# Hybrid decoder trunk: output-projection rows parked in DRAM through the expert stage, two more weight buffers, returned rows on SP's queue

## Chip, cores and metric

One core of one Trainium2 chip runs the whole kernel. The metric is the device time of one execution in microseconds; before the change it is 566.47 us (median of 3 runs, 566.22 to 566.54).

## What is computed

The reference, cut to what matters here (512 tokens, width 1024, 32 experts of which each token takes two):

```python
h = x + mix @ w_out                                   # output projection, mix from three mixers
h = h + hier_moe(rmsnorm(h, norm2_g), ...)            # 2 of 32 gated-MLP experts per token
gate = sigmoid(rmsnorm(h, ple_norm_g) @ ple_gate_w + ple_gate_b)
h = h + gate * (p @ ple_proj_w)
return rmsnorm(h, final_norm_g)
```

All is float32, and each expert's three matrices are 1024x256, 1024x256 and 256x1024: 3 MB an expert, 96 MB in all, read once.

## The kernel before

Tokens lie in four blocks `t` of 128 rows. `mixers` computes the mixers and adds the output projection to x; the sums stay in four SBUF tiles `h1[t]` of 128x1024 (4 KB a partition each). The rest is `ffn`, in these stages.

**Routing.** For each block, `route` (a generator, L782 on) normalizes h1[t], writes the normalized rows to DRAM tensor `tnd` by a DMA on the ACT queue (L790), and chooses experts. `spread` multiplies h1 by a selection to make the first expert pair's input; it is the last reader of h1 before the tail.

**Expert stage.** A loop over 16 pairs of experts, `i` = 0 to 15. `gate_up(i)` (line L997) multiplies by the two gate/up matrices, `down(i)` (L1029) by the two down matrices. A pair's output rows are scattered by token into DRAM tensor `yd` with an indirect DMA on POOL (L1043), for all pairs but the last; the next pair's input rows are gathered from `tnd` (L943).

**The weight stream.** The 96 MB come in 96 units of 1 MB. `load_units` (L691) takes a free buffer (a "slot") from the list `ring`, first in, first out, and issues the unit's DMA on SP's queue. SP's instructions stand in program order, so an issue that waits for a slot holds back all behind it. A manual dependency makes each unit wait until the third unit before it has landed, so three are in flight at most (`AHEAD = 3`). `free` puts slots back after each half of a pair. A pair's six units come in the order gate/up first halves, gate/up second halves, down, down.

**The end of the expert stage.** After `down(14)`, SP issues four 1 MB loads of the gate weights (`gate_load`, L1060) and two broadcast rows (L1190, L1191). POOL issues the four `load_y(t)` (L1162), each 1 MB: the two rows per token that the experts returned, read back from `yd`. They wait for the last scatter to land. From pair 14 on, the order on ACT and DVE is the program's, written by hand.

**The hand-over.** After `down(15)`: `add_y(0)` adds y's two rows to h1[0] (L1158, DVE, two instructions); `scatter` adds the last pair's output through two matmuls (L1051) and two DVE adds (L1053); `turn(0, hf)` transposes h1[0] (L1213) and copies it out (ACT L1215, DVE L1216). Between them stand twelve leftover steps of the per-layer embedding, `ple(4)` three times (PE L724, ACT copy L735). `split_gate(k, hf)` splits a piece of the raw gate weights into a high part (ACT L1068) and a low part (DVE L1069): 16 pieces, k = 0 to 7 for each half of the columns. Four are done ahead of the last `ple(4)`, twelve behind it. Then come the sigmoid table's load (L1309), `rms(0)` (ACT L1221, DVE L1202) and the tail: four blocks of gate matmuls (L1234), `finish` and the output. Blocks 1 to 3 get their `add_y` and `scatter` inside the tail.

The splits are the piece of code that the order of the end hangs on:

```python
    down(15, behind_down)              # behind_down: split_gate(0..2, 0), add_y(0)
    ple(PLE_LAST[0])
    for hf in range(2):
        scatter(hf)
    split_gate(3, 0)
    ple(PLE_LAST[1])
    lo = [turn(0, hf) for hf in range(2)]
    ple(PLE_LAST[2])
```

Of the kernel before, what the change touches and what calls it, by code (L numbers as in the profile page):

```python
# [38 lines left out]
def bcast(ap, parts=P):  # L39

    return bass.AP(tensor=ap.tensor, offset=ap.offset, ap=[[0, parts]] + [list(a) for a in ap.ap])
# [47 lines left out]
def mixers(ctx, tc, A, K, dbg):  # L89
# [360 lines left out]
    sbctx.close()  # L450
    pctx.close()
    hp = ctx.enter_context(tc.tile_pool(name="hp", bufs=1, side="left"))
    h1 = K["h1"] = [hp.tile([P, D], F32, name=f"h1_{t}") for t in range(NT)]
    for t in range(NT):
        nc.sync.dma_start(h1[t], A["x"][t * P:(t + 1) * P, :])
    parts = (step for t in range(NT) for hf in range(2) for step in out_proj(nc, K, mixh, mixl, hf, t, WO_EARLY))
# [157 lines left out]
def ffn(ctx, tc, A, K, mixh, mixl, out, dbg, stage):  # L614
# [21 lines left out]
    def unit(dt, shape, slot=None):  # L636
        slot = slot or ring.pop(0)
        u = slot[0].tile(shape, dt, name="unit", tag=slot[1])
        slot_of[id(u)] = slot, u
        return u  # L640
# [41 lines left out]

    slab, loads = {}, []

    def load_units(m=96):

        while ring and m and len(slab) < 96:
            n, m = len(slab), m - 1
            n = n - n % 6 + (0, 3, 1, 4, 2, 5)[n % 6]
            slab[n] = unit(F32, [P, 2048])  # L690
            loads.append(nc.sync.dma_start(slab[n], A["w_exp"][n // 3, n % 3]).ins)  # L691
            if len(loads) > AHEAD:
                tc.add_manual_dep(loads[-1], loads[-1 - AHEAD].name,
                                  mybir.DependencyInfo(mybir.DependencyClass.Sync, mybir.DependencyReason.DATA))
# [15 lines left out]
    def ple_load():  # L710
        pl_in.extend((big(0), unit(F32, [P, 2, D])))
        nc.sync.dma_start(pl_in[0], A["pT"])
        nc.sync.dma_start(pl_in[1], A["ple_proj_w"])

    def ple_steps():

        pT, pW = pl_in
        for j in range(8):
            t, hf = j // 2, j % 2
            p = ps("pe", "sc")  # L720
            for c in range(2):
                for k in range(2):
                    n = hf * 512 + c * 256
                    PE.matmul(p[:, c * 256:c * 256 + 256], pT[:, k * S + t * P:k * S + (t + 1) * P], pW[:, k, n:n + 256],  # L724
                              start=(k == 0), stop=(k == 1))
                    if c == k == 1:
                        kept.append((t, hf, p))
                        ple_out()
                    yield
# [9 lines left out]
    def ple(n):  # L739
        for _ in range(n):  # L740
            next(ple_left, None)
# [2 lines left out]
    V.tensor_copy(cm.rearrange("p a b -> p (a b)"), cmf)  # L744
    V.tensor_tensor(rw, rw, g2c[:, :, None].to_broadcast([P, KC, 36]), ALU.mult)
    tnd = dram.tile([S, D], F32, name="tnd")
    Ab = mw.tile([P, NT, 32], BF, name="Ab")
    pr_ = cw.tile([P, 448], F32, name="pr", tag="cmf")
    posA = pr_[:, :128].rearrange("p (t e) -> p t e", t=NT)
# [32 lines left out]
    def route(t):  # L782

        (ms2, hT, pl), ms = rt_in[t], small("ms", 1)
        V.tensor_tensor(ms, ms2[:, 0:1], ms2[:, 1:2], ALU.add)
        V.tensor_scalar(ms, ms, 1.0 / D, EPS, ALU.mult, ALU.add)
        r = rt_r[t] = rsqrt_cols(nc, mw, ms, 1, f"rs2{t}", K)
        tn = big(t % 2)
        SC.activation(tn, h1[t], AF.Copy, scale=r)
        nc.scalar.dma_start(tnd[t * P:(t + 1) * P, :], tn)  # L790
        yield

        lg = small("lg", 32)
        V.scalar_tensor_tensor(gp[:, t, :4], pl[:, :4], r, rb[:, :4], ALU.mult, ALU.add)
        V.scalar_tensor_tensor(lg, pl[:, 4:36], r, rb[:, 4:], ALU.mult, ALU.add)
        yield
        g8, gi = small("g8", 8, bufs=3), small("gi", 8, U32)
        V.max(g8, gp[:, t])
        yield
        V.max_index(gi, g8, gp[:, t])  # L800
        yield
        gf, oh = small("gf", 1), small("oh4", 4)
        V.tensor_scalar(gf, gi[:, 0:1], 8.0, None, ALU.mult)
        yield
        V.tensor_scalar(oh, iota32[:, 0:32:8], gf, None, ALU.is_equal)
        yield

        pr, ein = small("pr", 32), small("ein", 8)
        V.tensor_tensor(pr.rearrange("p (g e) -> p g e", g=4), lg.rearrange("p (g e) -> p g e", g=4),
                        oh[:, :, None].to_broadcast([P, 4, 8]), ALU.mult)  # L810
        yield
        V.tensor_reduce(ein, pr.rearrange("p (g e) -> p e g", g=4), AX, ALU.add)
        yield
        e8, ei = small("e8", 8, bufs=3), small("ei", 8, U32)
        V.max(e8, ein)
        yield
        V.max_index(ei, e8, ein)
        yield
        id2 = small("id2", 2, bufs=3)
        V.tensor_scalar(id2, ei[:, 0:2], gf, None, ALU.add)  # L820
        yield

        c0 = small("c0", 32, bufs=3)
        V.tensor_scalar(c0, iota32, id2[:, 0:1], None, ALU.is_equal)
        yield
        V.scalar_tensor_tensor(Ab[:, t], iota32, id2[:, 1:2], c0, ALU.is_equal, ALU.add)
        chosen[t] = g8, e8, id2, c0
# [104 lines left out]
    def one_hot(i, t):  # L932

        if t == 0:
            Dm[i] = mw.tile([P, NT, 2, 64], BF, name="Dm", tag="Dm")
        V.tensor_tensor(Dm[i][:, t], iota64[:, None, :].to_broadcast([P, 2, 64]),
                        posA[:, t, 2 * i:2 * i + 2, None].to_broadcast([P, 2, 64]), ALU.is_equal)
# [120 lines left out]
    def gate_load(j):  # L1058
        gr.append(unit(F32, [P, 4, 512]))
        nc.sync.dma_start(gr[j], A["ple_gate_w"][j])  # L1060

    def split_gate(k, hf):

        if hf == 0:
            gw[k] = unit(F32R, [P, 2, D])
        hs = slice(hf * 512, hf * 512 + 512)
        raw, h, l = gr[2 * hf + k // 4][:, k % 4], gw[k][:, 0, hs], gw[k][:, 1, hs]
        SC.activation(h, raw, AF.Copy, scale=g3c[:, k:k + 1])  # L1068
        V.scalar_tensor_tensor(l, raw, g3c[:, k:k + 1], h.bitcast(F32), ALU.mult, ALU.subtract)  # L1069
        if k % 4 == 3:  # L1070
            free(gr[2 * hf + k // 4])
# [3 lines left out]
    with tc.manual_schedule(engines={mybir.EngineType.DVE}):  # L1075
        run(steps[0])
        for t in (0, 1):
            hot_rms(t)
        logits(NT - 1, 1)
        run(steps[1], 3)  # L1080
        position(NT - 2)
        spread(0)
        run(steps[1], 2)
        hot_rms(NT - 2)
        spread(1)
        run(steps[1])
        spread(2)
        position(NT - 1)
        hot_rms(NT - 1)
        for t in range(3):  # L1090
            one_hot(1, t)
        spread(NT - 1)
        for hf in range(2):
            gather_T(0, hf)
        one_hot(1, NT - 1)
    ple_load()
    load_units()

# [56 lines left out]
    def add_y(t, rs=(0, 1)):  # L1155

        for r in rs:
            V.tensor_tensor(h1[t], h1[t], ys[t][:, r], ALU.add)  # L1158

    def load_y(t):  # L1160
        ys.append(unit(F32, [P, 2, D]))
        nc.gpsimd.dma_start(ys[t], yd.rearrange("(r n) d -> n r d", r=2)[t * P:(t + 1) * P])  # L1162

    ends = ExitStack()
    for i in range(16):
        if i == 14:
            ends.enter_context(tc.manual_schedule(engines={mybir.EngineType.Activation, mybir.EngineType.DVE}))
        gate_up(i, between(i))
        free(slab[6 * i + 1], slab[6 * i + 4])
        if i == 15:  # L1170
            break
        if i in (3, 7):
            eo.append(unit(F32, [P, 2, D]))
            ple_out()
        load_units()
        if i == 0:
            ple(PLE[0])
        gather_T(i + 1, 1)
        if i > 0:
            ple(PLE[i])  # L1180
        down(i, lambda n: gather_T(i + 1, 0))
        free(slab[6 * i + 2], slab[6 * i + 5])
        load_units()
        if i == 14:
            for t in range(NT):
                load_y(t)
            for j in range(4):
                gate_load(j)
            rows = mix.tile([P, 2, D], F32, name="rows", tag="m0")
            nc.sync.dma_start(rows[:, 0], bcast(A["ple_gate_b"]))  # L1190
            nc.sync.dma_start(rows[:, 1], bcast(A["final_norm_g"]))  # L1191


    free(slab[92], slab[95])
# [85 lines left out]
        for hf in range(2):  # L1280
            scatter(2 * t + hf)

    def behind_down(n):
        if n == 0:
            for k in range(3):
                split_gate(k, 0)
            add_y(0, (0,))
        if n == 1:
            add_y(0, (1,))

    down(15, behind_down)
    ple(PLE_LAST[0])
    for hf in range(2):
        scatter(hf)
    split_gate(3, 0)
    ple(PLE_LAST[1])
    lo = [turn(0, hf) for hf in range(2)]
    ple(PLE_LAST[2])
    free(pl_in[1])
    for f in lo:  # L1300
        f()
    for k in range(4, KC):
        split_gate(k, 0)
    count_beyond()
    for k in range(KC):
        split_gate(k, 1)
    ov_slots = ring[:3]
    junk, h3s = (unit(F32, shape, slot) for shape, slot in zip(([P, 2, 512], [P, 4, 512]), ring[3:]))
    SC.preload_act_table_set("sigmoid_and_others")  # L1309
# [160 lines left out]
```

## Time and profile before

| | us |
|---|---|
| median of 3 runs | 566.47 |
| the profiled execution, its own time | 564.66 |
| its span, first to last instruction | 562.9 |
| PE busy in the span | 517.0 |
| DVE busy | 276.7 |
| ACT busy | 210.6 |

Times in the rows count from the start of the span, on the slowest (here the only) core. PE is TensorE's matmuls, PEld its weight loads; an engine's name with a q is its instruction queue. The profiled execution lies 1.81 us below the median of the runs, and its span 1.76 us below its own time. The granted TensorE clock is 0.983 of full speed over the span.

### The profile page before, as it was taken

The page shows a single profiled execution, that of the slowest core. Times are in us where ns is not written, and L with a number is a line of the kernel's source. Part 1 is how long each engine was busy: PE and PEld are TensorE (multiplying, and loading weights), DVE is VectorE, ACT ScalarE, POOL GpSimd, SP SyncE. Part 2 cuts the span into 40 slices and gives each one's busy share as a digit, 9 for nine tenths or more (in the row PEclk, how much of TensorE's full clock was granted, in tenths as well). Part 3 has the DMA queues.
Part 4 walks back from the last instruction along what each step waited for, and adds up shares of the span by engine and source line. Part 5 has one row for each costly group of instructions (what it writes and reads, how often), then busy time and mean ns, then how long its engine had stood idle before and what let it go on. Part 6 is the DMA issues. An engine that isn't in the chain of part 4 may idle for free. (4 is left out here: it accounts for less than half of the span.)

```text
span 562.9 us, 7588 instructions
## 1 busy us (share of the span) xinstructions
PE 517.0 (92%) x2713; PEld 325.5 (58%) x2713; DVE 276.7 (49%) x735; ACT 210.6 (37%) x443; POOL 90.3 (16%) x126
## 2 busy tenths in 40 slices
PE   8999999999999999999999999988798897659992
PEld 5797886877996888853333333332223332448872
DVE  6663966847745667673222232221211112487764
ACT  7466765555856444211121111111011113173352
POOL 3301121311009300011111121100111002011110
PEclk9999999999999999999999999999999999788998
DMA  9881222300549589989999999999999999900111
GB/s 312 272 315 55 75 80 75 86 1 2 146 164 421 198 322 421 334 343 397 411 414 418 392 381 376 374 399 381 391 392 419 419 412 418 401 6 0 39 47 69
DMA packets 35641, 148.82 MB, mean 264 GB/s; under 512 B 6557, under 2 KB 14109, under 8 KB 22160
## 3 DMA queue, kind: packets, MB, share of 16 engines
q1 hardware_dynamic: 28896, 133.26, 61.8%
q0 software_dynamic: 5408, 12.15, 5.5%
q10 hardware_dynamic: 1296, 2.89, 1.3%
q8 instruction: 23, 0.38, 0.3%
q14 instruction: 18, 0.15, 0.1%
HBM read 139.61 MB, written 16.25 MB: 277 GB/s over the span
## 5 line engine op out<-in xcount | busy, mean ns | idle before, releaser
L997 PE MATMUL gu<-unit,xT 128*64 128x512 f32 x512 | 127.6, 598 | 12.4 <-DMA unit<-in_w_exp_dram 12.2
L997 PEld LDWEIGHTS gu<-unit,xT 128*64 128x64 f32 x512 | 37.1, 136 | 84.0 <-issue 59.0
L1029 PE MATMUL dn<-unit,hidT 128*64 128x512 f32 x256 | 61.0, 599 | 1.7 <-ACT hidT L1020 0.8
L234 PE MATMUL pj<-xh,wp 128*128 128x512 f32 x176 | 51.2, 398 | 0.4 <-ACT wp L69 0.4
L1234 PE MATMUL pg<-unit 128*128 128x512 f32 (+1 forms) x216 | 47.4, 376 | 1.1 <-ACT unit L1215 1.1
L1002 ACT ACTIVATE sg<-gu 128x256 f32<-128x256 f32 x16 | 6.2, 385 | 110.6 <-PE gu L997 110.6
L1003 DVE SCALAR_TENSOR_TENSOR hid<-sg,wsl,gu 128x256 f32<-128x256 f32 x16 | 7.7, 479 | 79.7 <-ACT sg L1002 79.7
L1234 PEld LDWEIGHTS pg<-unit 128*128 128x128 f32 x216 | 37.7, 192 | 9.0 <-ACT unit L1215 1.6
L1043 POOL DMA_INDIRECT yd<-big,idy x15 | 15.2, 1013 | 164.4 <-ACT big L1033 164.4
L1029 PEld LDWEIGHTS dn<-unit,hidT 128*64 128x64 f32 x256 | 19.1, 136 | 33.1 <-issue 24.5
L234 PEld LDWEIGHTS pj<-xh,wp 128*128 128x128 f32 x176 | 32.5, 188 | 8.0 <-ACT wp L69 1.1
L1033 ACT ACTIVATE big<-dn 128x512 f32<-128x512 f32 x30 | 17.9, 597 | 50.5 <-PE dn L1029 50.5
L930 DVE COPY SL<-sl 128x10 f32<-128x10 f32 (+1 forms) x17 | 2.9, 168 | 66.4 <-PE sl L929 66.4
L70 DVE TENSOR_TENSOR wp<-wraw,wp 128x768 fp32r<-128x768 f32 (+2 forms) x28 | 25.8, 928 | 13.7 <-ACT wp L69 13.4
L69 ACT ACTIVATE wp<-wraw 128x768 fp32r<-128x768 f32 (+2 forms) x28 | 22.8, 816 | 20.2 <-PE pj L234 9.8
L234 PE MATMUL pj<-xl,wp 128*128 128x512 f32 x88 | 29.4, 400 | 0.0
L986 DVE TENSOR_TENSOR xT<-xt,g2c 128x512 f32<-128x512 f32 x30 | 20.6, 688 | 11.8 <-PE xt L985 11.7
L80 PE MATMUL po<-wo,mx 128*128 128x512 f32 x96 | 25.7, 408 | 0.0
L257 PE MATMUL pj<-wp,xh 128*128 128x384 f32 x96 | 24.8, 351 | 0.0
L80 PE MATMUL po<-unit,mx 128*128 128x512 f32 x96 | 24.1, 399 | 0.0
L943 POOL DMA_INDIRECT xg<-tnd,idx x15 | 15.5, 1036 | 33.5 <-issue 15.8
L985 PEld LDWEIGHTS xt<-ident,xg 128*128 128x128 f32 x120 | 13.4, 140 | 11.5 <-issue 11.4
(294 smaller groups left out, 888.7 us busy)
## 6 DMA issues: line engine op xcount, KB each, us to landing
unit<-in_w_exp_dram SPq DMA_DIRECT2D x96, 1024.0 KB, 8.6
wraw<-in_w_in_dram SPq DMA_DIRECT2D x20, 384.0 KB, 3.5
yd<-zero SPq DMA_DIRECT2D x4, 1024.0 KB, 8.6
unit<-in_ple_gate_w_dram SPq DMA_DIRECT2D x4, 1024.0 KB, 15.0
unit<-yd POOLq DMA_DIRECT2D x4, 1024.0 KB, 19.3
wraw<-in_w_out_dram SPq DMA_DIRECT2D x8, 256.0 KB, 3.0
h<-in_x_dram SPq DMA_DIRECT2D x4, 512.0 KB, 5.2
unit<-in_w_out_dram SPq DMA_DIRECT2D x4, 512.0 KB, 9.2
```

Of the source, the lines that this page charges most:

```text
L69: nc.scalar.activation(h, src, AF.Copy)
L70: nc.vector.tensor_tensor(l, src, h.bitcast(F32), ALU.subtract)
L80: nc.tensor.matmul(p, a[k][:, ts_], K["wo"][k][:, b, hs], start=(n == 0), stop=(n == 3 * len(ks) - 1))
L234: PE.matmul(q, a[:, i * P:(i + 1) * P], b[k], start=(n == 0), stop=(n == 3 * KC - 1))
L257: PE.matmul(p[t][:, :W_IN[j]], a[k][:, t * P:(t + 1) * P], b, start=(n == 0), stop=(n == 3 * KC - 1))
L943: G.indirect_dma_start(out=xg[i % 2], out_offset=None, in_=tnd, in_offset=bass.IndirectOffsetOnAxis(ap=idx[:, i:i + 1], axis=0), bounds_ch ...
L986: V.tensor_tensor(xTs[i, hf], p.rearrange("p (a b) -> p a b", a=4), g2c[:, 4 * hf:4 * hf + 4, None].to_broadcast([P, 4, P]), ALU.mult)
L997: PE.matmul(gu[64 * e:64 * e + 64], xTs[i, k // 4][:, k % 4, 64 * e:64 * e + 64], w[e][k // 4][:, 512 * (k % 4):512 * (k % 4) + 512], star ...
L1029: PE.matmul(dn[64 * e:64 * e + 64], hT[:, f, 64 * e:64 * e + 64], w[e][2][:, 1024 * f + 512 * hf:1024 * f + 512 * hf + 512], start=(f == 0 ...
L1033: SC.activation(o[:, 512 * hf:512 * hf + 512], dn, AF.Copy)
L1043: G.indirect_dma_start(out=yd, out_offset=bass.IndirectOffsetOnAxis(ap=idy[:, i:i + 1], axis=0), in_=o, in_offset=None, bounds_check=2 * S ...
L1234: PE.matmul(p, hT[t][:, a, ks], gw[k][:, b, hs], start=start and n == 0, stop=stop and n == len(ab) - 1)
```

## The change

1. The four h1 tiles become two buffers of two rows each, `h0` and `h1`. `route` writes each finished h1[t] to a new DRAM tensor `hd` (ACT queue, behind the write to `tnd`). After `spread`, the two buffers join `ring` as slots for weight units.
2. `load_h(t)` reads h1[t] back from `hd` on SP's queue, into a slot taken from the ring (one slot for two blocks). h1[0] is read back before the last two of the 96 units; the others later.
3. `load_y` goes from POOL's queue to SP's. After `down(14)` SP's order is: y0, the four gate loads, h1[1], y1, a row, h1[2], y2, a row, h1[3], y3.
4. `split_gate` is cut into `gate_hi` (ACT) and `gate_lo` (DVE). None of it stands within `down(15)` any more: pieces 0 and 1 stand around the scatter and the turn, the other 14 behind the last `ple(4)`.
5. The last three psum tiles of the embedding use the banks of `gate_up` instead of those of `scatter`.

```diff
+    K["hp"] = hp
+    hh = [hp.tile([P, 2, D], F32, name=f"h1_{j}", tag=f"h{j}") for j in range(2)]
+    h1 = K["h1"] = [hh[t // 2][:, t % 2] for t in range(NT)]
-    h1 = K["h1"] = [hp.tile([P, D], F32, name=f"h1_{t}") for t in range(NT)]
...
+    def load_h(t):
+
+        if t % 2 == 0:
+            back.append(unit(F32, [P, 2, D]))
+        h1[t] = back[-1][:, t % 2]
+        nc.sync.dma_start(h1[t], hd[t * P:(t + 1) * P, :])
...
         while ring and m and len(slab) < 96:
+            if len(slab) == 94 and not back:
+                load_h(0)
+                continue
...
-            p = ps("pe", "sc")
+            p = ps("pe", "sc" if j < 5 else "gu")
...
+    hd = dram.tile([S, D], F32, name="hd")
...
         nc.scalar.dma_start(tnd[t * P:(t + 1) * P, :], tn)
+        nc.scalar.dma_start(hd[t * P:(t + 1) * P, :], h1[t])
...
+    ring.extend(((K["hp"], "h0"), (K["hp"], "h1")))
     ple_load()
     load_units()
...
-        nc.gpsimd.dma_start(ys[t], yd.rearrange("(r n) d -> n r d", r=2)[t * P:(t + 1) * P])
+        nc.sync.dma_start(ys[t], yd.rearrange("(r n) d -> n r d", r=2)[t * P:(t + 1) * P])
...
         if i == 14:
-            for t in range(NT):
-                load_y(t)
+            load_y(0)
             for j in range(4):
                 gate_load(j)
+            load_h(1)
+            load_y(1)
             rows = mix.tile([P, 2, D], F32, name="rows", tag="m0")
             nc.sync.dma_start(rows[:, 0], bcast(A["ple_gate_b"]))
+            load_h(2)
+            load_y(2)
             nc.sync.dma_start(rows[:, 1], bcast(A["final_norm_g"]))
+            load_h(3)
+            load_y(3)
...
-    def behind_down(n):
-        if n == 0:
-            for k in range(3):
-                split_gate(k, 0)
-            add_y(0, (0,))
-        if n == 1:
-            add_y(0, (1,))
-
-    down(15, behind_down)
+    down(15, lambda n: n < 2 and add_y(0, (n,)))
     ple(PLE_LAST[0])
+    gate_hi(0, 0)
     for hf in range(2):
         scatter(hf)
-    split_gate(3, 0)
+    gate_lo(0, 0)
+    gate_hi(1, 0)
     ple(PLE_LAST[1])
     lo = [turn(0, hf) for hf in range(2)]
     ple(PLE_LAST[2])
     free(pl_in[1])
     for f in lo:
         f()
-    for k in range(4, KC):
-        split_gate(k, 0)
+    gate_lo(1, 0)
+    for k in range(2, KC):
+        gate_hi(k, 0)
+        gate_lo(k, 0)
     count_beyond()
     for k in range(KC):
-        split_gate(k, 1)
+        gate_hi(k, 1)
+        gate_lo(k, 1)
```

## Rows read from the trace of the kernel before

**Rows 1.** The page, DMA share of the span in 40 slices, in tenths.

```profile
DMA  9881222300549589989999999999999999900111
```

**Rows 2.** Who waited for whom, PE alone, 360 to 472 us (total, times, longest).

```profile
PE gu L997 <- DMA unit<-in_w_exp_dram: 12.2, 11, 2.0
```

**Rows 3.** Stretches: busy us of each engine, granted clock, DMA share, GB/s.

```profile
200.00:226.00 26.00, 26.00 (x151) 22.42 (x150) 16.87 (x70) 12.22 (x30) 1.65 (x3) 1.00 0.95 394
226.00:230.00 4.00, 3.78 (x23) 3.06 (x21) 2.62 (x14) 0.41 (x2) 0.00 (x0) 1.00 0.80 263
...
243.00:248.00 5.00, 4.87 (x25) 1.46 (x22) 4.36 (x27) 2.14 (x7) 1.30 (x1) 1.00 0.62 215
248.00:260.00 12.00, 11.43 (x63) 5.63 (x64) 5.97 (x30) 1.96 (x4) 2.20 (x3) 1.00 1.01 395
...
400.00:460.00 60.00, 52.84 (x233) 20.96 (x234) 9.41 (x30) 8.23 (x17) 5.07 (x5) 1.00 1.01 412
```

**Rows 4.** The weight stream's own waits on SP's queue, 232 to 300 us.

```profile
SPq L691 <- DMA unit<-in_w_exp_dram: 46.0, 17, 8.2
SPq L691 <- PE gu L997: 8.9, 4, 4.9
```

**Rows 5.** ACT's DMA queue: packets, MB, share of 16 engines' span; the issues of one line.

```profile
q10 hardware_dynamic: 1296, 2.89, 1.3%
...
L790 ACTq DMA_DIRECT2D tnd<-big x4: 326/326/331, 208.9 to 234.5; - x4
```

**Rows 6.** The weight stream's line, 456 to 470 us: issues, and time to landing.

```profile
L691 SPq DMA_DIRECT2D unit<-in_w_exp_dram x3: 327/328/328, 458.0 to 463.6; - x3
...
DMA to landing us min/median/max: 8.0/8.0/8.2
```

**Rows 7.** Stretch of the last transfers, 472 to 482 us.

```profile
472.00:482.00 10.00, 5.81 (x25) 2.69 (x25) 2.42 (x4) 4.39 (x8) 0.30 (x1) 1.00 1.01 417
```

**Rows 8.** Chain that ended last, in order of time: start, us, what.

```profile
469.37 12.27 DMA unit<-yd
```

**Rows 9.** DMA issues of the page: KB each, median us to landing.

```profile
unit<-in_ple_gate_w_dram SPq DMA_DIRECT2D x4, 1024.0 KB, 15.0
unit<-yd POOLq DMA_DIRECT2D x4, 1024.0 KB, 19.3
```

**Rows 10.** Timeline of the hand-over, 472 to 503 us.

```profile
472.32 3.65 PE L1029 MATMUL dn<-unit,hidT 128*64 128x512 f32 x16 [0.47 <-ACT hidT L1020]
...
475.91 1.99 PE L724 MATMUL pe<-unit,big 128*128 128x256 f32 x8
...
481.66 1.23 DVE L1158 TENSOR_TENSOR h<-h,unit 128x1024 f32<-128x1024 f32 x1 [4.56 <-DMA unit<-yd]
...
485.87 3.73 PE L724 MATMUL pe<-unit,big 128*128 128x256 f32 x8
...
489.43 1.04 PE L1213 MATMUL xt<-ident,h 128*128 128x128 f32 x8
...
490.30 1.89 PE L724 MATMUL pe<-unit,big 128*128 128x256 f32 x8
...
492.23 0.60 ACT L735 ACTIVATE unit<-pe 128x512 f32<-128x512 f32 x1 [1.03 <-PE pe L724]
492.73 7.46 ACT L1068 ACTIVATE unit<-unit,g3c 128x512 fp32r<-128x512 f32 x12
...
502.86 0.16 DVE L1202 SCALAR_TENSOR_TENSOR ms<-pm,ms 128x1 f32<-128x1 f32 x1 [0.46 <-ACT unit L1221]
```

**Rows 11.** Stretch of the scatter and the embedding's leftover steps, 482 to 490 us.

```profile
482.00:490.00 8.00, 5.95 (x17) 4.11 (x18) 5.16 (x7) 0.37 (x1) 0.00 (x0) 0.57 1.02 409
```

**Rows 12.** Two rows of one buffer loaded apart: the reader, and the loads' landings.

```profile
171.09 1.06 ACT L676 ACTIVATE unit<-unit 128x1024 fp32r<-128x1024 f32 x1 [0.67 <-DMA unit<-in_w_out_dram]
...
L674 SPq DMA_DIRECT2D unit<-in_w_out_dram x4: 437/440/483, 163.5 to 164.9; - x4
...
DMA to landing us min/median/max: 7.6/9.2/10.7
```

More of the change, by code (lines that the diff above doesn't have):

```diff
@@ L683, in ffn @@
     slab, loads = {}, []
+    def load_h(t):
[3 more added lines that the diff above has]
+        nc.sync.dma_start(h1[t], hd[t * P:(t + 1) * P, :])
+    back = []
     def load_units(m=96):
         while ring and m and len(slab) < 96:
+            if len(slab) == 94 and not back:
+                load_h(0)
+                continue
             n, m = len(slab), m - 1
@@ L1060, in gate_load, with gate_part, gate_hi, gate_lo @@
         nc.sync.dma_start(gr[j], A["ple_gate_w"][j])
-    def split_gate(k, hf):
+    def gate_part(k, hf):
+        hs = slice(hf * 512, hf * 512 + 512)
+        return gr[2 * hf + k // 4][:, k % 4], gw[k][:, 0, hs], gw[k][:, 1, hs]
+    def gate_hi(k, hf):
         if hf == 0:
             gw[k] = unit(F32R, [P, 2, D])
-        hs = slice(hf * 512, hf * 512 + 512)
-        raw, h, l = gr[2 * hf + k // 4][:, k % 4], gw[k][:, 0, hs], gw[k][:, 1, hs]
+        raw, h, _ = gate_part(k, hf)
         SC.activation(h, raw, AF.Copy, scale=g3c[:, k:k + 1])
+    def gate_lo(k, hf):
+        raw, h, l = gate_part(k, hf)
         V.scalar_tensor_tensor(l, raw, g3c[:, k:k + 1], h.bitcast(F32), ALU.mult, ALU.subtract)
```

## The prediction

> **What bounds the kernel now.** I read the slices first: from the 16th slice to the 35th, 211 to 492 us, the 16 DMA engines are full but for one slice of 8 [rows 1]. So half of the span could be bound by bytes. The waits of PE say from when on it is: from 360 us to the last unit, PE waits 11 times for expert weights, 12.2 us in all [rows 2]. The table of stretches shows the rate that goes with it: 412 GB/s at a full share from 400 to 460 us [rows 3]. There the arrival of a unit sets the time; before 360 us the read-ahead still covers, and what PE loses there it has back by waiting less.
>
> The last unit is issued at 463.6 us and lands 8.0 us later, at 471.6 [rows 6]; the last down matmuls start at 472.32, at once behind it [rows 10]. Then comes a second bound, of order. The first y transfer, y0, is issued by POOL at 469.37, behind the last scatter, and takes 12.27 us [rows 8], because SP put four gate loads on the same engines from 463.9 us; DVE waits 4.56 us for it [rows 10]. PE has little to do meanwhile, and its clock falls: 0.57 granted from 482 to 490 us [rows 11], a mix of the levels 2.4 and 1.2 GHz. The eight embedding matmuls at 485.87 take 3.73 us, where the same eight take 1.99 and 1.89 before and behind them [rows 10]. ACT's copy at 492.23 waits for the last of them, and twelve splits stand in a row behind it, 7.46 us, before the chain goes on with the tail [rows 10].
>
> **The change, part by part.**
>
> *Writing hd.* Four transfers of 0.5 MB on ACT's queue, 2.10 MB. That queue moved 2.89 MB at 1.3% of 562.9 us, which is 7.3 us of all engines, so 2.10 MB cost 5.3 us of DMA. They follow the four writes of the same size to `tnd`, issued from 208.9 to 234.5 us [rows 5]. Two holes lie there: 0.20 of 4 us at 226 and 0.38 of 5 us at 243, together 2.7 us [rows 3].
>
> *Two more slots.* The stream's own stalls for slots, 8.9 us in four waits for PE behind 232 us [rows 4], are mostly not idle DMA, since units are then still in flight; what is idle is the second hole, and two units to fetch there close it. Behind 248 us the share is 1.01 [rows 3], and more slots can't make it move more. So I take both holes as filled, and the stream ends 5.3 - 2.7 = **2.6 us later**. Bounds: everything idle from 200 us on, 1.3 us more (0.05 of 26 us), gives 1.3; nothing filled gives 5.3. Four more issues on ACT (0.33 us each by those of `tnd` [rows 5]) hold up the routing, but PE's 12.2 us of later waiting [rows 2] cover that; without that cover they would cost 1.3 us.
>
> *h1[0] in front of the last two units.* 0.52 MB at 412 GB/s: **1.3 us**. The last down unit lands at 471.6 + 2.6 + 1.3 = 475.5. The gate/up units ahead of it are only 2.6 late, so `down(15)` then waits for its weights, no longer for `hid`.
>
> *y on SP's queue, ahead of the gates.* SP's y0 waits for the last scatter as POOL's did, so it is issued at 469.4 + 2.6 = 472.0 and holds back all gate loads till then. Units are in flight till 475.5, so the engines don't run dry: y0's 1.05 MB land 2.5 us behind the last unit at 417 GB/s [rows 7], at 478.0. Before it was 469.37 + 12.27 = 481.64: **3.6 us earlier**. Behind it come four gates (to 488.1), h1[1], y1 (491.9) and the rest, 3.9 us more bytes than before in all with h1[0]; the tail asks for y1 only when the chain is past its DVE row at 502.86 [rows 10], so some 7 us are left.
>
> A rule bears on these prices. The rows show 412 to 417 GB/s in full stretches [rows 3, 7]. The Trainium skill, "DMA: Bandwidth & Descriptors", section "Bandwidth", says that between HBM and SBUF the HBM side binds at about 358 GB/s a core. By it hd, h1[0] and y0 would cost 5.9, 1.5 and 2.9 us, 1.2 more together, and the sum below would be -2.7 instead of -3.9. I go by the rows.
>
> *PE at full clock.* DVE adds y, corrects and scatters; in the trace the second embedding group starts 4.23 us behind y0 (485.87 against 481.64), and I keep that: 482.2. `down(15)` ends at 475.5 + 3.65 = 479.2, the first group fills to 481.1, the scatter follows; PE has no hole of over 2 us, so I expect no fall of the clock. Then 1.99 for the group, 1.04 for the transposes, 1.89 for the third group, less overlaps of 0.1: 4.8 us instead of 492.23 - 485.87 = 6.36: **1.6 us saved**. The other bound is a clock that falls all the same: nothing saved.
>
> *The splits.* Fourteen instead of twelve behind the last copy, 7.46 / 12 = 0.62 each: **1.2 us added**. The two ahead of it need gate 0, at 480.6, and stand in ACT's order before the copies of the turn; those want to run at 484.7, so 4 us are left. The banks of the last three embedding tiles cost nothing: `gate_up` has no pair left, and PE order stays. The last gate lands 488.1, and its splits come at 493 at the earliest.
>
> **Sum:** -3.6 (y0) - 1.6 (clock) + 1.2 (splits) = **-4.0**; I round the overlaps down to **-3.9**. The sum is against the profiled execution, 564.66 us with a span of 562.9; the span becomes 559.0. The median of the runs lies 1.81 above that execution, so the time is 566.47 - 3.9 = 562.6.
>
> **Rivals.**
>
> *A. The read-ahead pays for itself.* Holes in the table are averages; if also the idle share before 226 us and thin spots behind 248 us are used, the stream ends no later: -3.9 - 2.6 = -6.5, **560.0 us**. For it: 8.9 us of waits for slots, more than I count as idle [rows 4]. Against it: the share behind 248 us is already 1.01.
>
> *B. The holes stay.* The write of the last rows of hd holds the two slots up past 248 us, since a slot is free only when its rows are written out, and SP's order keeps the next units behind them. Then 5.3 us count in full: -3.9 + 2.7 = -1.2, **565.3 us**, at the edge of no change. For it: the transfers of that kind wait among full queues. Against it: a unit in flight covers SP's wait.
>
> *C. The queue gives y0 nothing; slower.* In the trace four SP loads issued together land after a median of 15.0 us, and y after 19.3 on its own queue [rows 9]: who is issued into a full machine waits. If y0 still takes 12.27 us on SP, it lands at 472.0 + 12.27 = 484.3, 2.7 later than before, and the sum is 2.7 - 1.6 + 1.2: +2.3, **568.8 us**. It decides from y0 at 482.0 on, where the 4.0 us are used up. Against it: units issued behind one another on SP land in order, 8.0 us each with three in flight [rows 6]. The Trainium skill, same page, section "Issuing engines are not separate DMA queues", states the general form: all queues share the engines and a second one saves only issue time. By that rule the move as such brings no rate; what I count on is the place in SP's order.
>
> *D. The two rows in one buffer count as one.* If DVE's add on h1[0] waits for all of its buffer, it waits for h1[1], which lands at 488.1 + 1.3 = 489.4 behind the gates, 7.8 us later than y0 did: about +7.4, **573.9 us**. Against it: the first of the four loads of the output projection's late weights is read at 171.09, when it landed (163.5 + 7.6), and its neighbour in the same buffer, issued some 0.5 us later, could not have landed before 171.6 [rows 12].
>
> **How the numbers follow.** Forecast 0.55, A 0.14, B 0.15, C 0.12, D 0.04. Differences up to 0.2% (1.1 us) can't be told from none here. The forecast's own bounds are 1.3 and 5.3 for the stream and 1.6 for the clock: -5.2 to about -1.2, all faster; A is faster, B half faster and half the same, C and D slower. That gives 0.76 faster, 0.08 same, 0.16 slower. The range reaches from A, with some room for the noise of the runs, over the forecast and B to a little past no change: 559.5 to 566.3, which leaves out C and D.
>
> **What would show it.** Right: hd's writes at a full share between 226 and 248 us and no hole at 243; the last unit's issue some 3 to 4 us later than 463.6; one y landing about 2.5 us behind it; DVE's first add of y at 478; three embedding groups of 2 us each with a granted clock of 1.00; fourteen splits in a row from 487; the DVE row of 502.86 near 499. Wrong: a last unit later than 477.5 (B and beyond), y0 at 482 or later (C), a DVE wait that ends with h1's load (D), ACT waiting for gate 0 ahead of the turn, or a tail that gives back what the hand-over gained.

## The result, and the profile after

The changed kernel takes 559.34 us (median of 13 runs, 556.75 to 562.66) beside 565.61 for the kernel before on the same chip (13 runs, 563.64 to 567.51). The ratio is 0.9896 with an interval of 0.9875 to 0.9917: 5.9 us faster (the two medians lie 6.3 apart), and 0.9896 x 566.47 = 560.6 us by the runs the prediction started from. The direction was right and the time lies in the range, but the gain is 5.9 us where 3.9 were forecast, and the time is nearer to rival A's 560.0 than to the forecast's 562.6. The profiled execution took 561.21 us, with a span of 559.5.

Executions must be lined up before their rows are compared. The first row here is the first DVE copy of the mixer's state in the timeline of the kernel before, the next the stretch of its first 40 us (columns as in [rows 3]):

```profile
173.79 0.42 DVE L533 COPY ST<-pkv 128x96 f32<-128x96 f32 x2 [1.74 <-PE pkv L529]
```

```profile
0.00:40.00 40.00, 36.98 (x174) 30.75 (x175) 27.54 (x40) 25.89 (x38) 9.26 (x12) 1.00 0.85 301
```

and the same two of the changed kernel:

```profile
176.27 0.42 DVE L535 COPY ST<-pkv 128x96 f32<-128x96 f32 x2 [1.71 <-PE pkv L531]
```

```profile
0.00:40.00 40.00, 36.64 (x161) 29.78 (x162) 27.12 (x39) 25.36 (x37) 9.24 (x12) 0.96 0.85 296
```

Ahead of that copy only the placing of the h1 tiles was changed, yet it stands 2.48 us later; the granted clock of the first 40 us was 0.96 instead of 1.00. It is the execution and not the change: e1 and e9 below are the same code and have the copy at 174.04 and 177.09. So 2.5 us are taken off every time of this trace before it is held against one of before ("lined up" below).

The chain that ended last in the changed kernel (start, us, what) has the 94th weight unit, the last one ahead of h1[0], and y0 (which answers to [rows 8]):

```profile
460.26 7.44 DMA unit<-in_w_exp_dram
...
471.78 7.44 DMA unit<-yd
```

Two stretches of it, the second answering to [rows 11]:

```profile
472.00:475.00 3.00, 1.59 (x6) 0.70 (x8) 0.48 (x1) 0.75 (x2) 0.00 (x0) 1.00 0.77 291
482.00:490.00 8.00, 6.55 (x33) 5.41 (x34) 5.72 (x10) 4.92 (x9) 0.00 (x0) 1.00 1.01 418
```

And its timeline of the hand-over (start, us, engine, line), which answers to [rows 10]:

```profile
473.85 4.39 PE L1045 MATMUL dn<-unit,hidT 128*64 128x512 f32 x16 [0.47 <-ACT hidT L1036]
474.59 0.30 PEld L1045 LDWEIGHTS dn<-unit,hidT 128*64 128x64 f32 x4 [0.56 <-DMA unit<-in_w_exp_dram]
478.17 1.99 PE L738 MATMUL pe<-unit,big 128*128 128x256 f32 x8
479.25 1.22 DVE L1181 TENSOR_TENSOR unit<-unit 128x1024 f32<-128x1024 f32 x1 [6.37 <-DMA unit<-yd]
483.20 1.89 PE L738 MATMUL pe<-unit,big 128*128 128x256 f32 x8
485.80 1.89 PE L738 MATMUL pe<-unit,big 128*128 128x256 f32 x8
487.72 0.60 ACT L749 ACTIVATE unit<-pe 128x512 f32<-128x512 f32 x1 [1.02 <-PE pe L738]
488.22 8.69 ACT L1087 ACTIVATE unit<-unit,g3c 128x512 fp32r<-128x512 f32 x14
499.59 0.16 DVE L1230 SCALAR_TENSOR_TENSOR ms<-pm,ms 128x1 f32<-128x1 f32 x1 [0.46 <-ACT unit L1249]
```

y0 is in at 479.22, lined up 476.7, which is 4.9 us earlier than 481.64 [rows 8, 10]. From y0 to ACT's last embedding copy it takes 8.50 us (487.72 - 479.22), before 10.59 (492.23 - 481.64): 2.1 us saved, with the clock at 1.00 where [rows 11] have 0.57 and with groups of 1.9 us where [rows 10] have 3.73. From that copy to DVE's ms row it takes 11.87 instead of 10.63: 1.2 us given back, by fourteen splits in 8.69 us for twelve in 7.46. Together -5.8, and behind the ms row nothing changes: 59.9 us remain to the end of the span, before 60.0.

In this one execution y0 landed 4.67 us behind the last unit (which landed at 474.55, and PE's weight loads go on at 474.59), and the engines ran thin just behind y0's issue at 471.78 (share 0.77 from 472 to 475). The issue was not late: it stands 2.8 us ahead of the last unit's landing, and in e1 below, where y0 follows 2.54 us behind that unit, 2.7 us ahead. A second execution of the same kernel, run e5 below, doesn't have that hole. Its stretch, the chain's row of its 94th unit, and its timeline:

```profile
472.00:475.00 3.00, 2.87 (x12) 1.61 (x14) 0.00 (x0) 0.29 (x2) 0.00 (x0) 1.00 1.04 426
```

```profile
458.48 7.51 DMA unit<-in_w_exp_dram
```

```profile
472.82 2.34 PEld L1045 LDWEIGHTS dn<-unit,hidT 128*64 128x64 f32 x13 [0.50 <-DMA unit<-in_w_exp_dram]
475.34 1.22 DVE L1181 TENSOR_TENSOR unit<-unit 128x1024 f32<-128x1024 f32 x1 [4.18 <-DMA unit<-yd]
483.82 0.60 ACT L749 ACTIVATE unit<-pe 128x512 f32<-128x512 f32 x1 [1.02 <-PE pe L738]
495.69 0.16 DVE L1230 SCALAR_TENSOR_TENSOR ms<-pm,ms 128x1 f32<-128x1 f32 x1 [0.46 <-ACT unit L1249]
```

There y0 lands 2.55 us behind the last unit (475.32 against 472.77), and the chain goes through PE's down matmuls and the embedding, no longer through y. Its copy of the state stands at 174.23, so 0.44 us come off.

The stretches around the holes, in the changed kernel, answer to [rows 3]:

```profile
226.00:230.00 4.00, 4.00 (x31) 3.60 (x29) 2.98 (x14) 1.68 (x5) 0.00 (x0) 1.00 1.01 422
230.00:243.00 13.00, 11.80 (x101) 11.05 (x101) 8.81 (x47) 2.84 (x5) 0.54 (x1) 1.00 0.93 358
243.00:248.00 5.00, 5.00 (x30) 2.06 (x31) 4.13 (x21) 2.13 (x7) 1.24 (x1) 1.00 1.02 426
248.00:260.00 12.00, 10.84 (x60) 5.10 (x58) 6.83 (x34) 1.37 (x4) 0.99 (x1) 1.00 1.01 419
```

Its waits on SP's queue from 232 to 300 us (total, times, longest) answer to [rows 4]:

```profile
SPq L705 <- DMA unit<-in_w_exp_dram: 51.2, 19, 6.6
SPq L726 <- DMA tnd<-big: 8.5, 1, 8.5
```

ACT's DMA queue on its page answers to [rows 5]:

```profile
q10 hardware_dynamic: 1872, 4.99, 2.3%
```

Both holes are filled (1.01 and 1.02 instead of 0.80 and 0.62; 1.02 in both when the stretches are lined up). The stream's long waits for PE (8.9 us in [rows 4]) are gone, and another wait has grown to 8.5 us from 2.2: SP's load at L726 waits for the last normalized rows, whose write now queues behind hd. It keeps the weight stream's next issue till 239.05 us, and a new hole opens there: the share from 230 to 243 us is 0.93, where the kernel before has 1.00, so 0.9 us of DMA are idle that were not:

```profile
230.00:243.00 13.00, 12.01 (x103) 10.55 (x105) 8.88 (x45) 2.66 (x5) 0.55 (x1) 1.00 1.00 381
```

The queue's share rose by 1.0% of 559.5, 5.6 us for 2.1 MB, as priced.

### The profile page after: what moved, and what is told of

The parts are those of the page before. It is cut to its first block, busy times and chain, and to the rows that moved or that the text cites. A ratio compares the mean times of both kernels' runs of the same rounds, so it can differ in the third digit from the quotient of the medians.

```text
span 559.5 us, 7601 instructions
## 1 busy us (share of the span) xinstructions
PE 518.5 (93%) x2713; PEld 329.0 (59%) x2713; DVE 277.2 (50%) x735; ACT 211.1 (38%) x443; POOL 86.3 (15%) x122
## 4 chain that ended last, share of the span: by engine, by line
PE 57%; DMA 25%; DVE 8%; ACT 6%; issue 2%; POOL 1%; SPq 0%; ACTq 0%; DVEq 0%; POOLq 0%
DMA unit<-in_w_exp_dram 19%; PE gu L1013 10%; PE pj L234 9%; PE po L80 8%; PE dn L1045 5%; PE pj L257 5%; PE z L257 4%; PE z L311 2%; PE po L333 2%; ACT unit L1087 2%; DVE unit L1181 2%; DMA xg<-tnd,idx 1%; PE x L990 1%; DMA unit<-yd 1%; PE pl L795 1%
## 5 line engine op out<-in xcount | busy, mean ns | idle before, releaser
L1013 PE MATMUL gu<-unit,xT 128*64 128x512 f32 x512 | 127.9, 598 | 10.9 <-DMA unit<-in_w_exp_dram 10.9
L234 PE MATMUL pj<-xh,wp 128*128 128x512 f32 x176 | 52.5, 406 | 0.3 <-ACT wp L69 0.3
L1045 PEld LDWEIGHTS dn<-unit,hidT 128*64 128x64 f32 x256 | 21.2, 136 | 31.2 <-issue 20.4
```

The source lines that it names most:

```text
L234: PE.matmul(q, a[:, i * P:(i + 1) * P], b[k], start=(n == 0), stop=(n == 3 * KC - 1))
L1013: PE.matmul(gu[64 * e:64 * e + 64], xTs[i, k // 4][:, k % 4, 64 * e:64 * e + 64], w[e][k // 4][:, 512 * (k % 4):512 * (k % 4) + 512], star ...
L1045: PE.matmul(dn[64 * e:64 * e + 64], hT[:, f, 64 * e:64 * e + 64], w[e][2][:, 1024 * f + 512 * hf:1024 * f + 512 * hf + 512], start=(f == 0 ...
```

## The experiments

All ratios are to the kernel before, run beside the kernel on the same chip; the kernels of one group below shared a chip. The changed banks (part 5) stay in every run.

### First group: which part of the change gains

**e1, the end alone.** h1 stays in SBUF: no hd, no slots, no reading back. The new order of y and of the splits stays.

```diff
-    hh = [hp.tile([P, 2, D], F32, ...) for j in range(2)]
+    h1 = K["h1"] = [hp.tile([P, D], F32, name=f"h1_{t}") for t in range(NT)]
...
-            if len(slab) == 94 and not back:
-                load_h(0)
-                continue
...
-        nc.scalar.dma_start(hd[t * P:(t + 1) * P, :], h1[t])
-    ring.extend(((K["hp"], "h0"), (K["hp"], "h1")))
...
-            load_h(1)
...
-            load_h(2)
...
-            load_h(3)
```

> The changed kernel with h1 kept in SBUF: nothing written to or read back from DRAM, no added slots; only y on SP's queue in the new order, the splits and the banks as changed. Theory T (the hand-over alone makes the gain; slots, write and read-back together come to about nothing): y0 lands some 7.4 us after its issue, 4.5 to 5 us earlier than before, the last embedding group runs at full clock, two more splits stand behind it: 5 to 6.5 us faster than before, ratio 0.989 to 0.991. Rival R (the read-ahead makes a good part): 2.5 to 4 us faster, ratio 0.993 to 0.996. The prediction's sum, without its 3.9 us of delay of the last unit: 7.8 us faster, 0.986.

Measured: 556.36 us, ratio 0.9824 (0.979 to 0.9857). The part of the change that parks h1 isn't needed for the gain; without it the median is 9.4 us under before, more than any of the three expectations had. Its timeline of the hand-over:

```profile
471.94 3.65 PE L1039 MATMUL dn<-unit,hidT 128*64 128x512 f32 x16 [0.47 <-ACT hidT L1030]
473.76 1.23 DVE L1174 TENSOR_TENSOR h<-h,unit 128x1024 f32<-128x1024 f32 x1 [2.79 <-DMA unit<-yd]
482.82 0.60 ACT L744 ACTIVATE unit<-pe 128x512 f32<-128x512 f32 x1 [1.03 <-PE pe L733]
494.68 0.16 DVE L1220 SCALAR_TENSOR_TENSOR ms<-pm,ms 128x1 f32<-128x1 f32 x1 [0.46 <-ACT unit L1239]
```

**e2, the parking alone.** hd, the slots and the reading back stay; y goes back to POOL's queue, and the splits to their old places.

```diff
-        nc.sync.dma_start(ys[t], yd.rearrange(...)[t * P:(t + 1) * P])
+        nc.gpsimd.dma_start(ys[t], yd.rearrange(...)[t * P:(t + 1) * P])
-            load_y(0)
+            for t in range(NT):
+                load_y(t)
-    down(15, lambda n: n < 2 and add_y(0, (n,)))
+    down(15, behind_down)                 # split_gate(0..2, 0), add_y(0)
```

> The other half alone: h1 written to DRAM, two more slots, h1 read back on SP; but y on POOL's queue and the splits where they were before. T: no gain, 0 to 2 us slower than before (ratio 1.000 to 1.003), because the same first y wait stands behind more bytes. R: 2 to 3 us faster (0.995 to 0.997). The prediction's terms: the last unit 3.9 us late and nothing given back, 3.9 us slower (1.007).

Measured: 565.57 us, 0.9986 (0.9963 to 1.0009), no difference from before; the loss of 3.9 us that the prediction's terms give (1.007) lies outside the interval. y0 again takes 11.87 us on POOL's queue (issued 472.74), and the clock from 482 to 490 us is 0.63.

**e3, no slots.** The changed kernel, but the two buffers join the ring only at the end of pair 14, for the reading back.

```diff
-    ring.extend(((K["hp"], "h0"), (K["hp"], "h1")))      # after spread
         if i == 14:
+            ring.extend(((K["hp"], "h0"), (K["hp"], "h1")))
             load_y(0)
```

> The changed kernel, but the two buffers come back as slots only at the end of pair 14, so the weights have no more slots than before and the write and the read-back are paid all the same. If the slots pay for the write (about 2 us), 2 to 4 us slower than the changed kernel, 2 to 4 us faster than before (0.993 to 0.996). If the slots are worth nothing, as the changed kernel (0.989 to 0.991).

Measured: 560.68 us, 0.9874 (0.9833 to 0.9914), the same as the changed kernel. The hole is filled without the slots too, as the stretch of e3 shows (lined up, 246.57 to 251.57, it is at 1.01):

```profile
243.00:248.00 5.00, 5.00 (x34) 2.69 (x34) 3.59 (x19) 1.08 (x7) 0.24 (x1) 1.00 1.00 416
```

while in e1, which has neither slots nor write, it is open:

```profile
243.00:248.00 5.00, 5.00 (x27) 1.53 (x24) 4.40 (x28) 2.14 (x7) 1.25 (x1) 1.00 0.65 220
```

So it is the backlog of the write, not weight units fetched ahead, that lies there. Beside the write, the two slots are worth nothing that can be measured; what they would be worth without it isn't shown.

**e4, hd written twice.** A second copy that nobody reads.

```diff
         nc.scalar.dma_start(hd[t * P:(t + 1) * P, :], h1[t])
+        nc.scalar.dma_start(hd2[t * P:(t + 1) * P, :], h1[t])
```

> The changed kernel with each finished row block written to DRAM twice (2.1 MB more on ACT's queue). The prediction's price with no hole left: 5.3 us slower than the changed kernel, so about 0.5 to 1 us faster than before (0.998 to 0.999). If a write beside the weight stream costs what the stream's units show in the changed kernel's trace (1.1 to 1.7 us late from the 21st unit on): 1 to 2 us slower than the changed kernel (0.992 to 0.994).

Measured: 563.28 us, 0.9921 (0.9889 to 0.9953), which is the second expectation; the first (0.998) lies outside the interval. By the ratios that is 1.4 us above the changed kernel's 0.9896, and 2.7 above e3 on the same chip, with intervals that overlap. So a second 2.1 MB do cost something, but less than the 5.3 us that its bytes would cost at the queue's price. The stretch of e4 that is taken up again below:

```profile
198.80:261.80 63.00, 59.77 (x366) 44.68 (x366) 40.17 (x183) 21.35 (x47) 4.57 (x7) 1.00 0.97 397
```

### Second group: the parts of the end

**e5, the changed kernel again**, as the reference of its group.

> The changed kernel once more, for a second trace of it. If the first y's landing 4.7 us behind the last unit (against 2.5 us in the run with h1 kept in SBUF) belongs to the change, it is 4 to 5 us again; if it was that one execution's, about 2.5 us, with DVE's first add of y some 2 us earlier against the last unit. Ratio 0.987 to 0.992 either way.

Measured: 558.19 us, 0.9878 (0.9841 to 0.9916), with y0 2.55 us behind the last unit, as the second case of the expectation has it. Its rows stand above.

**e6, h1[0] behind the last two units**, directly ahead of y0.

```diff
-            if len(slab) == 94 and not back:
-                load_h(0)
-                continue
...
         if i == 14:
+            load_h(0)
             load_y(0)
```

> The changed kernel, but h1[0] is read back behind the last two weight units, between them and y0. If the first y's landing sets the hand-over (the bytes in front of it are the same), nothing changes against the changed kernel, within 0.5 us, though the last unit lands 1.3 us earlier. If the last down unit sets it, 1.0 to 1.3 us faster than the changed kernel.

Measured: 559.24 us, 0.988 (0.9843 to 0.9917), the same as e5. The last two units no longer have h1[0]'s bytes in front of them, but y0, which the chain needs next, has the same bytes in front of it as in e5. In its trace y0 lands 2.54 us behind h1[0] (479.96 against 477.42). Where the 0.5 MB stand ahead of y0 makes no difference that the times show.

**e7, e1 with y on POOL's queue.** The order of the splits stays new.

```diff
-        nc.sync.dma_start(ys[t], yd.rearrange(...)[t * P:(t + 1) * P])
+        nc.gpsimd.dma_start(ys[t], yd.rearrange(...)[t * P:(t + 1) * P])
-            load_y(0)
+            for t in range(NT):
+                load_y(t)
             for j in range(4):
                 gate_load(j)
```

> The run with h1 kept in SBUF, but y back on POOL's queue beside the gate loads, as before; so only the splits and the banks are changed. Theory T2 (the place of y0 in SP's order makes the gain): y0 lands some 12 us after its issue again, PE idles and its clock falls, and two more splits stand behind the last copy: 0 to 1.5 us slower than before (1.000 to 1.003). Rival (the new place of the splits frees ACT and DVE by itself): 2 us or more faster than before.

Measured: 566.23 us, 1.0007 (0.998 to 1.0035). All of e1's gain is gone. y0 is issued by POOL at 469.66 and lands 11.9 us later, DVE waits, PE runs dry, and the clock falls; the timeline of e7, then its stretch:

```profile
481.59 1.23 DVE L1174 TENSOR_TENSOR h<-h,unit 128x1024 f32<-128x1024 f32 x1 [10.88 <-DMA unit<-yd]
485.80 3.62 PE L733 MATMUL pe<-unit,big 128*128 128x256 f32 x8
```

```profile
482.00:490.00 8.00, 6.01 (x17) 4.38 (x18) 5.10 (x7) 0.55 (x1) 0.00 (x0) 0.57 1.02 408
```

**e8, e1 with the splits in their old places.** y stays on SP.

```diff
-    down(15, lambda n: n < 2 and add_y(0, (n,)))
+    down(15, behind_down)                 # split_gate(0..2, 0), add_y(0)
...
+    split_gate(3, 0)                      # behind the scatter; the loop from k = 4
```

> The run with h1 kept in SBUF and y on SP's queue ahead of the gates, but the splits where they were before, three of them within the last down step. T2 with ACT's order: those three wait for gate 0, which lands 2.5 us behind y0, and ACT's copies of the down output behind them come some 4 us late, so the run loses about 3 us against the run with the splits moved: 5.5 to 7.5 us faster than before (0.987 to 0.990). Rival (the splits' place does not matter): as that run, 0.980 to 0.985.

Measured: 562.31 us, 0.9947 (0.992 to 0.9974): a smaller gain than I had expected. Gate 0 now comes behind y0, so ACT, whose next instruction is the first split, waits for it with the copies of the down output behind it; PE runs dry here too, and the clock's fall was the part that I had left out. The timeline of e8, then its stretch:

```profile
477.55 1.95 ACT L1081 ACTIVATE unit<-unit,g3c 128x512 fp32r<-128x512 f32 x3 [5.21 <-DMA unit<-in_ple_gate_w_dram]
479.40 1.06 ACT L1048 ACTIVATE unit<-dn 128x512 fp32r<-128x512 f32 x2
484.50 3.48 PE L733 MATMUL pe<-unit,big 128*128 128x256 f32 x8
```

```profile
482.00:490.00 8.00, 7.32 (x26) 5.62 (x27) 4.67 (x8) 1.57 (x3) 0.00 (x0) 0.64 1.01 390
```

So the two edits of the end need each other: y first in SP's order makes the gates late, and late gates make the old places of the splits wrong. Alone they give 1.0007 (e7, splits) and 0.9947 (e8, y), together 0.9824 (e1).

### Third group: the price of the write, and a better end

**e9, e1 again; e10, the changed kernel again.**

> The run with h1 kept in SBUF once more, now beside the changed kernel on one chip. If writing, read-back and slots together cost 2 to 4 us, as the first comparison across two calls had it: 0.980 to 0.985, and 2 to 4 us under the changed kernel. If the first run was luck and they cost no more than the 0.8 us between two of the traces: 0.986 to 0.988.

> The changed kernel, for the comparison on one chip: 0.987 to 0.991. The first y 2.5 us behind the last unit, as in its second trace.

Measured: e9 557.54 us, 0.9852 (0.9815 to 0.989); e10 558.99 us, 0.9884 (0.9855 to 0.9912). The order is that of e1 and the changed kernel in the other groups. The medians of this group are 1.5 us apart and the intervals overlap; e1 and the changed kernel of the result, on two chips, are 4.1 apart by their ratios. So the parking costs some 1.5 to 4 us, not sharply settled.

**e11, e1 with hd written and never read.**

```diff
+        nc.scalar.dma_start(hd[t * P:(t + 1) * P, :], h1[t])
```

> The run with h1 kept in SBUF, plus the writes of h1 to DRAM, which nobody reads. The prediction's price of the write, 5.3 us less the holes of 2.7: 2.6 us slower than without. By the units in the traces that have the write, 1.0 to 1.5 us late from the 21st unit on: 1.0 to 1.5 us slower than without, and the rest of the way to the changed kernel, 1.3 us for h1[0] in front of the last two units, is the read-back.

Measured: 556.71 us, 0.9861 (0.9826 to 0.9895), beside e9's 0.9852. In the times the write by itself can't be told from none. It fills the hole of 243 to 248 us as in the changed kernel, here without slots; the stretch of e11:

```profile
243.00:248.00 5.00, 5.00 (x24) 1.44 (x20) 4.43 (x28) 2.14 (x7) 1.24 (x1) 1.00 1.02 428
```

**e12, e1 with four more split halves in the gaps ahead of the last copy.**

```diff
     gate_hi(1, 0)
+    gate_hi(2, 0)
     ple(PLE_LAST[1])
+    gate_lo(1, 0)
     lo = [turn(0, hf) for hf in range(2)]
+    gate_hi(3, 0)
     ple(PLE_LAST[2])
...
-    gate_lo(1, 0)
-    for k in range(2, KC):
+    gate_lo(2, 0)
+    gate_lo(3, 0)
+    for k in range(4, KC):
```

> The run with h1 kept in SBUF, with four pieces of the gate weights split ahead of the last copy of the embedding instead of two, in ACT's idle time behind the scatter and the turn. If ACT's row of splits sets the way to the tail, two fewer behind the copy save 2 x 0.62 = 1.2 us: 1.2 us faster than without. If DVE's low parts set it, nothing.

Measured: 554.43 us, 0.9804 (0.9773 to 0.9834), 10.9 us under before in its group and the fastest version of the study. Its timeline:

```profile
482.96 0.60 ACT L744 ACTIVATE unit<-pe 128x512 f32<-128x512 f32 x1 [0.42 <-PE pe L733]
483.45 7.46 ACT L1081 ACTIVATE unit<-unit,g3c 128x512 fp32r<-128x512 f32 x12
493.59 0.16 DVE L1220 SCALAR_TENSOR_TENSOR ms<-pm,ms 128x1 f32<-128x1 f32 x1 [0.46 <-ACT unit L1239]
```

From the copy to the ms row it takes 10.63 us, where e1 takes 11.86 (494.68 - 482.82): the 1.2 us of the two more splits are had back. The medians of e12 and e9 lie 3.1 us apart; the traces don't show where the rest comes from, and by the ratios e1, on another chip, is only 1.1 us behind e12.

## Why the prediction was right, and where it was short

**The stream, "2.6 us later": the term that was mis-sized.** Lined up, the 31st unit is issued between 274.1 and 274.3 us in the six traces without the write (before, e1, e7, e8, e9, e12) and between 275.1 and 276.8 in the seven with one write (the changed kernel, e2, e3, e5, e6, e10, e11). That is 1.4 us later on average, and the two kinds don't mix. Here is that issue in e1 and then in e11, which differ by the write alone (0.25 and 0.40 us come off):

```profile
L700 SPq DMA_DIRECT2D unit<-in_w_exp_dram x1: 328/328/328, 274.4 to 274.4; - x1
```

```profile
L700 SPq DMA_DIRECT2D unit<-in_w_exp_dram x1: 328/328/328, 275.9 to 275.9; - x1
```

Later on, single traces scatter more. The 94th unit should have landed 2.6 us later than before; lined up it lands at 465.2 in the changed kernel (467.70 - 2.48) and at 465.6 in e5 (465.99 - 0.44), against 466.2 before (458.0 + 8.2 [rows 6]): earlier, if anything. But that trace of before is the latest of its six: they reach from 464.1 to 466.2, with a mean of 465.2, and the seven with the write from 464.9 to 468.8 (e6), with a mean of 466.1. So write and slots cost the stream some 0.9 to 1.4 us where the forecast had 2.6; the timed runs of e11 and e9, 0.0009 apart, are too wide to say it. For the same reason the last down unit, which by the forecast lands 3.9 us later than before, lands lined up only 0.5 us later (474.55 - 2.48 against 471.58), and 0.8 and 0.9 in e5 and e10.

Three things in the step were wrong. First, the slots: I let units fetched ahead fill the second hole, and e3 fills it without slots. Second, the write opened a new hole of 0.9 us while it filled the old ones. Third, and of more weight, I took a full share for a fixed rate ("more slots can't make it move more"). The same 63 us of the kernel before, and then of the changed one, lined up, say otherwise:

```profile
197.00:260.00 63.00, 61.09 (x374) 45.52 (x374) 41.47 (x189) 21.24 (x47) 5.69 (x8) 1.00 0.92 358
```

```profile
199.50:262.50 63.00, 60.64 (x370) 45.15 (x370) 40.01 (x184) 21.24 (x47) 5.43 (x7) 1.00 0.95 385
```

The share rises by 0.03, 1.9 us, but the rate by 27 GB/s, which over 63 us is 1.7 of the added 2.1 MB. In the last 12 us the share is 1.01 in both, at 395 and (lined up) at 417 GB/s. Only 0.4 MB were left to push the weights back, 1.0 us at 412 GB/s, and the 31st unit of this trace is 1.1 us late. e4 answers to the same account: its 63 us ran at 397 GB/s, which is 0.8 MB more for a second 2.1; 1.3 MB are left, 3.3 us, and its 31st unit stands at 278.9, lined up, 3.3 us behind the mean of the seven. Why a full share moves more with the writes among the loads is open.

**h1[0], 1.3 us: right.** From the 94th unit to the last one it takes 6.85 us in the changed kernel (474.55 - 467.70) and 6.78 in e5, where e1 takes 5.40: 1.4 more. `down(15)` waits for its weights, as forecast: its sixteen matmuls take 4.39 us instead of 3.65.

**y0 2.5 us behind the last unit: right** in e5 and e10 (2.55 each), e3 and e1 (2.54 each), nearly so in e9, e11 and e12 (2.7 to 2.9); the 4.67 of the first trace is its own hole. With the last unit 3.1 us less late than forecast, y0 gains 6.8 us in e5 (481.64 against 475.32 - 0.44) for the 3.6 forecast, and the difference is just the stream's. Of the 3.1, by the means of the 94th unit, 1.7 are the write's smaller cost, 1.0 is that the trace of before runs late, and the rest is e5's own.

The stretch of 472 to 475 us in e5 ran at 426 GB/s. So the 358 GB/s that the Trainium skill gives in "DMA: Bandwidth & Descriptors", section "Bandwidth", are not the price of these bytes here: the same section ties that rate to two cores streaming from one memory, and here one core runs. The measurement decides.

**The clock, 1.6 us: right in kind, 2.1 in size.** The granted clock is 1.00 where it was 0.57. The kernels in which PE runs dry ahead of the embedding (before, e2, e7, e8) all show 0.57 to 0.64 there, and groups of 3.5 to 3.7 us. The 0.5 us beyond the forecast are half in the chain from y0 to the second group, which I had kept at 4.23 us and which takes 3.98 (483.20 - 479.22), and half in the overlaps behind it.

**The splits, 1.2 us: right**, 1.24 measured, and e12 shows that it wasn't a must.

So the sum by the forecast's own steps with the measured stream is -3.9 - 3.1 - 0.5 = -7.5; e5 and e10 have it in their traces (ms row lined up 7.6 and 7.5 earlier) and are timed, by their ratios, at 6.9 and 6.6 us under before, near to the -6.5 that is left without the 1.0 us of the late trace of before. The first trace, at 5.8, has the hole behind the last unit on top; whether the thirteen runs beside it (5.9) had it too isn't shown.

**The rivals.** A's time nearly came, but not for A's reason: the read-ahead pays nothing (e3), and the stream is still about 1 us later. B's open holes didn't come. C is refuted: on SP y0 lands 5.2 us behind its issue in e1 (468.55 to 473.74), on POOL 11.9 in e7, where the gate loads are ahead of it. By the Trainium skill, "DMA: Bandwidth & Descriptors", section "Issuing engines are not separate DMA queues", another engine's queue brings no rate; the runs agree, since what SP's queue brought is the place ahead of the gates. In e1 all four y loads are on SP's queue:

```profile
DMA to landing us min/median/max: 5.2/16.6/19.0
```

The 5.2 us are y0's, ahead of the gates; the other three, behind them, take 15.0 to 19.0. No run has y0 on POOL's queue ahead of the gates, so that the place would do as much there isn't shown. D is refuted: DVE's first add starts when y0 lands (479.22, 479.25), while h1[1] is still behind the gates; in e10, where the add starts at 477.48, h1[1] lands at 488.7.

## What to carry to other kernels

When a stage ends on a transfer that everything waits for, put that transfer into the queue of the stream that fills the engines, directly behind the last part of it, and then check who wanted the transfers that it displaces: here the splits had to move with it, and each edit alone gave a third of what both gave, or nothing. Don't price added traffic as bytes at the full rate less idle time: a full DMA share moved 395 GB/s and then 417 in the same place, and the write cost the stream about 1 us where I had priced 2.6. And don't judge a microsecond of the stream by one trace on each side: the one trace of before was 1.0 us late among its kind. A buffer freed for reading ahead is worth what the read-ahead is short of, and here, with holes of 2.7 us in all that the write itself filled, that was nothing.

## What was not expected of the hardware

Executions of the same code differ at the start: the first copy of the mixer's state stands between 173.79 and 177.36 us over fourteen traces, and between 174.04 and 177.09 in two of the same code (e1, e9). The granted clock of the first 40 us goes with it: 1.00 in the traces that have it by 174.3, 0.96 between 175.5 and 176.3, 0.91 in the two behind 177 (e3 and e9). Differences of single traces below 3 us mean nothing until this is taken off.

In one of three profiled executions of the changed kernel the engines ran thin for 3 us exactly as y0 was issued (share 0.77 instead of 1.04), and y0 landed 2.1 us later behind the last unit than in the other two; e4, with its second write, has y0 3.3 us behind it. What causes it stays open.
